# Tile addresses and the transposition of probabilities in a retention and sparse-attention block

## The chip, the cores and the metric

The kernel runs on one core of a Trainium2 chip. Its time is the device time of one execution in microseconds; several executions are taken, and the median counts. Beside it a hardware profile of one execution shows what each engine did: TensorE (PE, with its weight loads as PEld), VectorE (DVE), ScalarE (ACT), GpSimd (POOL), and the DMA queues that SyncE (SP) and POOL feed.

## The reference, cut to what matters

One block of a model: a feed-forward half step, a mixer, a second feed-forward half step, on 16 meta tokens and 512 tokens of 1024 channels, in float32. The mixer adds two branches, each through a sigmoid gate: retention (4 heads, values of 512 channels) and attention (8 heads of 128) over 16 meta keys and the keys that an index picks.

```
def hybrid_mixer(u, pos, k_top, w_in, w_ret_out, w_att_out, w_mix_out):
    ...
    yr = retention(rq.transpose(0, 2, 1, 3), rk.transpose(0, 2, 1, 3), rv.transpose(0, 2, 1, 3))
    yr = yr.transpose(0, 2, 1, 3).reshape(B, T, RET_V)
    yr = (jax.nn.silu(rg) * yr) @ w_ret_out
    ...
    ya = dsa_attention(aq, ak, av, iq, ik, iw, k_top).reshape(B, T, ATT_W) @ w_att_out
    merged = jax.nn.sigmoid(g_ret) * yr + jax.nn.sigmoid(g_att) * ya
    return merged @ w_mix_out
...
        # dsa_attention, one block of queries
        s_meta = jnp.einsum('bqhd,bmhd->bhqm', qb, k_meta).astype(jnp.float32) * scale
        s_meta = jnp.where((meta_pos[None, :] <= tq[:, None])[None, None], s_meta, -jnp.inf)
        s_sel = jnp.einsum('bqhd,bqkhd->bhqk', qb, k_sel).astype(jnp.float32) * scale
        s_sel = jnp.where(sel_ok[:, None], s_sel, -jnp.inf)
        p = jax.nn.softmax(jnp.concatenate([s_meta, s_sel], axis=-1), axis=-1).astype(v.dtype)
        return (jnp.einsum('bhqm,bmhd->bqhd', p[..., :N_META], v_meta)
                + jnp.einsum('bhqk,bqkhd->bqhd', p[..., N_META:], v_sel))
```

## The kernel before, in words

Every large product is made of three: each float32 operand is split into a high part (`split`, L116: an ACT copy to the type fp32r) and a low part (L118: a DVE subtraction), and high x high, high x low and low x high are summed in PSUM (`mm3`, L142 to 157). Weights come by SP's queue into `raw`, and are split into `whi` (ACT) and `wlo` (DVE), each with three buffers.

The order of the work on TensorE is written out by hand: it is the order of the calls. In the attention heads the order on ACT, DVE and POOL is decided when the program is built, by a scheduler that places each instruction; inside a block `with tc.manual_schedule(engines=BUSY)` it is that of the calls too.

Retention keeps its tiles in the pool `rt` (opened at L1807): values `vo`, decayed scores `ph` and `pl`, and two tiles of tails, `vtail` and `ptail`, which hold the last 16 keys stacked for one product. Its weighted sums are `pspv` (L1476 to 1484) and its output projection `psro`. `gap(p, n)` (L273) puts a spacer of n floats into a pool, so that what follows it starts further on; `tails` (L1304) allocates the two tails.

Attention keeps its tiles in the pool `at`. The keys are counted with the 16 meta keys first, the queries without them; so a block of 128 keys, kb, is seen by the queries from 16 before its own block of 128 on. `KQ = [0, 112, 240, 256, 496]` gives the first query column that is kept for each kb: 512, 400, 272, 256 and 16 columns. For every head, in this order on TensorE:

- `score` (L1882): the scores `psS` of four blocks of queries, then DVE's reduction, ACT's exponential into `prob[j]`, and DVE's scaling. `prob[j]` holds 128 queries by 128(j+2) keys; its columns past the last admissible key are zeroed once, when it is allocated.
- `proj_q`, `proj_k`: the next head's queries and keys (`psaq`, `psak`, then `aq`, `ak`).
- `transpose_p` (L1913): the probabilities are turned, keys to partitions, into PSUM (`psPT`, four buffers shared with other small tiles), and split into `pth` and `ptl`. For kb the blocks j = kb-1 to 3 are turned, 13 in all; the block j = kb-1 has only its last 16 queries by 16 keys different from zero among the columns kept. A fourteenth turns the last 16 keys of j = 3, which go to `ptail` (`split_rows`, L1322 to 1326: two ACT copies and a DVE subtraction).
- `wide_gate`: the 24 products of a gate (`psgate`, later `psga`), which need the weights just split.
- `weigh_v` and `weighted` (L1476 to 1484): `psao`, twelve products of v with `pth`, `ptl`, `pth` for kb = 0 to 3, and one with `ptail`. Its result is split into the output `vo` of the pool `ao`, which the output projection `psat` reads after the last head.

Of the kernel before, what the change touches and what calls it, by code (L numbers as in the profile page):

```python
# [11 lines left out]
F32 = mybir.dt.float32  # L12
F32R = mybir.dt.float32r
# [5 lines left out]
P = 128  # L19
D = 1024  # L20
KD = D // P
S = 512
NM = 16
T = S + NM
# [24 lines left out]
KQ = [0, 112, 240, 256, 496]  # L49
# [32 lines left out]
def kernel(ctx: ExitStack, tc: tile.TileContext, x, meta, g1, wg1, wu1, wd1, gm,  # L82
                      w_in, w_ro, w_ao, w_mo, g2, wg2, wu2, wd2, gf, rope, decay, causal, out):
    nc = tc.nc
# [9 lines left out]
    def pool(name, bufs=1, space=None, side=None):  # L94
        kw = {} if space is None else {"space": space}
        if side is not None:
            kw["side"] = side
        return tc.tile_pool(name=name, bufs=bufs, reuse_waits="tile", **kw)
# [6 lines left out]
    ident = cpool.tile([P, P], F32, name="ident")  # L105
# [10 lines left out]
    def split(src, hi, lo, eng=nc.vector):  # L116
        nc.scalar.activation(hi, src, AF.Copy)  # L117
        eng.tensor_tensor(lo, src, hi.bitcast(F32), ALU.subtract)  # L118
# [85 lines left out]
    tp = {}  # L204
# [43 lines left out]
    def wide(n):  # L248

        return -(-n // 64) * 64  # L250
# [22 lines left out]
    def gap(p, n):  # L273

        nc.gpsimd.memset(p.tile([P, n], F32, tag=f"gap{n}", name="gap"), 0.0)
# [257 lines left out]
    def sm_tile(name):  # L533
        return mx["sm"].tile([P, S], F32, tag="sm", name=name)

    def mm_tile(name):
        return mx["mm"].tile([P, 1024], F32, tag="mm", name=name)
# [761 lines left out]
    def stacked(p, name, n):  # L1299
        t = p.tile([P, n], F32R, tag=name, name=name)  # L1300
        nc.gpsimd.memset(t[:TR].bitcast(F32), 0.0)
        return t

    def tails(p, n):  # L1304

        tp.update(v=stacked(p, "vtail", S), p=stacked(p, "ptail", n))
# [13 lines left out]
    def split_rows(src, t, order):  # L1320

        nc.scalar.activation(t[:NM], src, AF.Copy)  # L1322
        at = [32 * i for i in range(1, 3) if order[i] == "h"][0]
        nc.scalar.activation(t[at : at + NM], src, AF.Copy)
        at = 32 * order.index("l")
        nc.vector.tensor_tensor(t[at : at + NM], src, t[:NM].bitcast(F32), ALU.subtract)
# [26 lines left out]
    if True:  # L1353
# [393 lines left out]
        p = RH - 1  # L1747
# [20 lines left out]
        for h in range(1, RH):  # L1768
            gates = gates_of(h)
            n = 4 - (h == p)  # L1770
# [35 lines left out]
        rts = ExitStack()  # L1806
        rt = rts.enter_context(pool("rt"))  # L1807
        tp.update(pool=rt, bufs=4)
        gap(rt, 16)
        tails(rt, 64)  # L1810
        ia, ib = (rt.tile([P, 4, S], F32, tag=f"vo{i}", name="ixs") for i in range(2))
        ka, kb_ = tmp(), tmp()
# [9 lines left out]
        for c in range(2):  # L1822
            t = rt.tile([P, S], F32, tag="sg", name="gate", bufs=4)
# [17 lines left out]
    with pool("ao") as ao:  # L1841
        vo = [ao.tile([P, AH, S], F32R, tag=f"vo{i}", name="vo") for i in range(2)]
        ao_parts = [(vo[0][:, c, :], vo[1][:, c, :]) for c in range(AH)]
        with pool("at") as at:
# [3 lines left out]
            prob = []  # L1848
            for j in range(4):
                wj = min(P * (j + 2), T)  # L1850
                pj = at.tile([P, wj], F32, tag=f"pj{j}", name=f"pj{j}")
                if j < 3:
                    nc.gpsimd.memset(pj[:, NM + P * (j + 1) :], 0.0)
                prob.append(pj)
            tails(at, 48)
            cq, ck = (Cols(w_in, o_ + P, AH - 1, step=1) for o_ in (OFF_AQ, OFF_AK))
            scale = DH**-0.5

# [24 lines left out]
            def score(j, q, k):  # L1883
                n = NM + P * (j + 1)
                qs = slice(j * P, (j + 1) * P)
                if j < 3:
                    ps = sm_tile("psS")
                    outs = [(ps[:, : max(n, 256)], slice(0, max(n, 256)))]
                    sv = ps[:, :n]
                else:  # L1890
                    outs, sv = halves(mm_tile("psS3"))
                for i, (a, b) in enumerate(((q[0], k[0]), (q[0], k[1]), (q[1], k[0]))):
                    for o_, sl in outs:
                        nc.tensor.matmul(o_, a[:, qs], b[:, sl], start=i == 0, stop=i == 2)
                s = tmp()
                m = at.tile([P, 4], F32, tag="stat", name="stat", bufs=8)
                nc.vector.tensor_tensor_reduce(s[:, :n], sv, bias[j], 1.0, MARK, ALU.add,
                                               ALU.max, m[:, 0:1])
                nc.vector.tensor_scalar(m[:, 1:2], m[:, 0:1], -scale, None, ALU.mult)
                nc.scalar.activation(prob[j][:, :n], s[:, :n], AF.Exp, bias=m[:, 1:2], scale=scale,  # L1900
                                     accum_out=m[:, 2:3])

                def to_one():
                    nc.vector.reciprocal(m[:, 3:4], m[:, 2:3])
                    nc.vector.tensor_scalar(prob[j][:, :n], prob[j][:, :n], m[:, 3:4], None, ALU.mult)

                return to_one

            def scores(q, k):
                for j in (2, 1, 0, 3):  # L1910
                    score(j, q, k)()

            def transpose_p():  # L1913
                parts = []
                for kb in range(4):
                    ps = sm_tile("psPT")
                    for j in range(max(kb - 1, 0), 4):
                        nc.tensor.transpose(ps[:, j * P : (j + 1) * P], prob[j][:, kb * P : (kb + 1) * P], ident)
                    if kb == 3:
                        nc.tensor.transpose(ps[:NM, 0:P], prob[3][:, 4 * P : T], ident)  # L1920
                    n = S - KQ[kb]
                    ph = at.tile([P, wide(n)], F32R, tag=f"pth{kb}", name="pth")[:, :n]
                    pl = at.tile([P, wide(n)], F32R, tag=f"ptl{kb}", name="ptl")[:, :n]
                    if kb == 3:
                        split_rows(ps[:NM, P - NM : P], tp["p"][:, :NM], "hlh")
                    split(ps[:, KQ[kb] :], ph, pl)
                    parts.append((ph, pl))
                return parts

            def weigh_v(h, parts, v):  # L1930
                ps = mm_tile("psao")[:, :S]
# [11 lines left out]
            with tc.manual_schedule(engines=BUSY):  # L1943
                w = gr.next()
                k, q = rope_k(first_k, nc.vector), rope_q(first_q, nc.vector)
                t, t5 = (at.tile([P, S], F32, tag="gate", name="gate", bufs=2) for _ in range(2))
                nc.scalar.activation(t, first_gate, AF.Sigmoid)
                gate_acc(4, t)
                ps = mm_tile("psgate")[:, :S]
# [8 lines left out]
            for h in range(AH):  # L1958
                more = h + 1 < AH
                if h:  # L1960
                    scores(q, k)
                if more:
                    q, k = proj_q(w if h == 0 else None), proj_k()
                else:
                    wide_gate(sm_tile("psga"))
                    wide_gate()
                pt = transpose_p()
                wide_gate()
                weigh_v(h, pt, vs[h])
                if h == 1:  # L1970
                    with tc.manual_schedule(engines=BUSY):
                        more_vs = split_values(raw, [v[:, 4:, :] for v in vo])
                if h == 3:
                    place_tails(5)
                    vs += more_vs
# [6 lines left out]
        with pool("ou") as ou:  # L1982
# [6 lines left out]
            for c in range(KD):  # L1989
                w = cols.next()  # L1990
                ps = sm_tile("psat")
                mm3([(ps, slice(0, S))], w, lambda k: ao_parts[k], KD)
                if c < n_left:
                    t = ou.tile([P, S], F32, tag="sa", name="sa", bufs=3)
                    nc.scalar.dma_start(t, gd[KD + c])
                else:
                    t = sa[c - n_left]
# [12 lines left out]
    with pool("om") as ou:  # L2010
# [11 lines left out]
        for c in range(KD):  # L2022
# [3 lines left out]
            ps = sm_tile("psmo")  # L2026
# [254 lines left out]
```

## Time and profile before

| | us |
|---|---|
| median of three runs (1521.64 to 1523.09) | 1522.1 |
| the profiled execution | 1523.13 |
| its span in the trace | 1521.4 |
| PE busy | 1512.0 (99%) |
| PEld busy | 1369.5 (90%) |
| DVE busy | 1094.6 (72%) |
| ACT busy | 725.1 (48%) |
| POOL busy | 103.8 (7%) |
| the attention heads, in the trace | 910 to 1076 |

Times in the trace are counted from the start of the span. A matmul's start is when it begins; its end is modelled, since matmuls overlap in the array, so that the pace of a chain is read from start to start. A row of the timeline gives start, duration, engine, line, operation, written and read tiles, shape, and in brackets how long the engine sat idle before it and who ended that. The chain is a list of pieces: start, length, engine, tile, line and how many instructions.

### The profile page before, as it was taken

What the parts mean: (1) busy time and instruction counts of PE and PEld (TensorE: products, weight loads), DVE (VectorE), ACT (ScalarE), POOL (GpSimd) and SP (SyncE); (2) the same over time, 40 slices, a digit from 0 to 9 for tenths busy, and PEclk for the clock granted to TensorE, in tenths of its full rate; (3) what the DMA queues carried; (4) which work ended last, traced back from release to release, by engine and by line L of the source; (5) the groups of instructions that cost most, each with busy time, mean ns of one, the idle gap of its engine ahead of it and who ended that gap; (6) DMA issues with size and microseconds to landing.
All of it is one profiled execution on the core that took longest, in us unless ns stands there. A gap on an engine that the chain in (4) does not pass through costs nothing.

```text
span 1521.4 us, 23948 instructions
## 1 busy us (share of the span) xinstructions
PE 1512.0 (99%) x9797; PEld 1369.5 (90%) x9797; DVE 1094.6 (72%) x1679; ACT 725.1 (48%) x1132; POOL 103.8 (7%) x133
## 2 busy tenths in 40 slices
PE   9999999999999999999999999999999999999997
PEld 8999999999988888789888888998888899899996
DVE  4988586786886767787878787666455888586675
ACT  5655263454354444543334357666345445254453
POOL 1000000003101120000000021110002000000000
PEclk9999999999999999999999999999999999999999
DMA  5132323226554444232322233233433223233232
GB/s 168 58 121 89 118 90 111 91 92 211 191 167 162 165 146 142 86 122 85 112 82 85 96 118 94 78 88 109 148 131 131 83 84 106 89 111 111 84 124 84
DMA packets 151742, 173.50 MB, mean 114 GB/s; under 512 B 4944, under 2 KB 123240, under 8 KB 150992
## 3 DMA queue, kind: packets, MB, share of 16 engines
q1 hardware_dynamic: 142992, 151.58, 30.7%
q0 software_dynamic: 3808, 11.38, 2.0%
q10 hardware_dynamic: 4832, 9.00, 1.7%
q8 instruction: 77, 1.26, 0.3%
q14 instruction: 33, 0.27, 0.1%
HBM read 155.94 MB, written 16.01 MB: 113 GB/s over the span
## 4 chain that ended last, share of the span: by engine, by line
PE 99%; issue 0%; ACT 0%; DVE 0%; POOL 0%; POOLq 0%
PE psqX L157 14%; PE psd L157 8%; PE psd L2116 8%; PE psqY L157 7%; PE psrg L157 6%; PE psro L157 6%; PE psvX L1135 4%; PE psqZ L157 3%; PE psrk L157 3%; PE psak L157 3%; PE psu L157 3%; PE psrq L157 3%; PE psaq L157 3%; PE psga L157 3%; PE psat L157 3%; PE psmo L157 3%
## 5 line engine op out<-in xcount | busy, mean ns | idle before, releaser
L285 DVE TENSOR_TENSOR wlo<-raw,whi 128x1024 fp32r<-128x1024 f32 (+2 forms) x184 | 198.8, 1084 | 42.4 <-ACT whi L284 42.4
L284 ACT ACTIVATE whi<-raw 128x1024 fp32r<-128x1024 f32 (+2 forms) x184 | 169.8, 924 | 123.3 <-PE psd L157 41.3
L157 PE MATMUL psqX<-tl,whi 128*128 128x264 f32 (+1 forms) x432 | 122.3, 283 | 0.0
L157 PE MATMUL psqX<-th,whi 128*128 128x264 f32 (+1 forms) x432 | 122.3, 283 | 0.0
L157 PE MATMUL psqX<-th,wlo 128*128 128x264 f32 (+1 forms) x432 | 122.2, 283 | 0.0
L118 DVE TENSOR_TENSOR wlo<-raw,whi 128x1024 fp32r<-128x1024 f32 (+1 forms) x60 | 73.6, 1226 | 54.3 <-ACT whi L117 51.8
L284 ACT ACTIVATE whi<-wsum 128x1024 fp32r<-128x1024 f32 x72 | 76.3, 1060 | 70.7 <-PE psd L2116 22.0
L117 ACT ACTIVATE whi<-raw 128x1024 fp32r<-128x1024 f32 (+1 forms) x60 | 62.3, 1043 | 87.8 <-PE psat L157 26.6
L285 DVE TENSOR_TENSOR wlo<-wsum,whi 128x1024 fp32r<-128x1024 f32 x72 | 87.8, 1221 | 12.5 <-ACT whi L284 12.5
L157 PEld LDWEIGHTS psqX<-th,whi 128*128 128x128 f32 x432 | 82.1, 190 | 0.1
L157 PEld LDWEIGHTS psqX<-th,wlo 128*128 128x128 f32 x432 | 82.0, 190 | 0.0
L157 PEld LDWEIGHTS psqX<-tl,whi 128*128 128x128 f32 x432 | 82.0, 190 | 0.0
L157 PE MATMUL psro<-vo,whi 128*128 128x512 f32 x256 | 79.4, 391 | 0.0
L157 PE MATMUL psd<-hl,whi 128*128 128x264 f32 x352 | 71.4, 284 | 0.0
L157 PE MATMUL psd<-hh,wlo 128*128 128x264 f32 x352 | 70.8, 283 | 0.0
L157 PE MATMUL psd<-hh,whi 128*128 128x264 f32 x352 | 70.6, 282 | 0.0
L2116 PE MATMUL psd<-wlo,hh 128*128 128x512 f32 (+1 forms) x182 | 69.3, 382 | 0.0
L2116 PE MATMUL psd<-whi,hh 128*128 128x512 f32 (+1 forms) x182 | 69.2, 382 | 0.0
L2116 PE MATMUL psd<-whi,hl 128*128 128x512 f32 (+1 forms) x182 | 69.2, 382 | 0.0
L157 PEld LDWEIGHTS psro<-vo,whi 128*128 128x128 f32 x256 | 48.1, 188 | 10.3
L157 PEld LDWEIGHTS psd<-hh,wlo 128*128 128x128 f32 x352 | 54.5, 188 | 0.0
L157 PEld LDWEIGHTS psd<-hh,whi 128*128 128x128 f32 x352 | 54.1, 188 | 0.0
(451 smaller groups left out, 4514.4 us busy)
## 6 DMA issues: line engine op xcount, KB each, us to landing
raw<-in_ffn_w_up_dram SPq DMA_DIRECT2D x22, 1024.0 KB, 4.9
raw<-in_ffn_w_gate_dram SPq DMA_DIRECT2D x21, 1024.0 KB, 5.0
raw<-in_w_in_dram SPq DMA_DIRECT2D x18, 1024.0 KB, 5.0
raw<-in_w_in_dram SPq DMA_DIRECT2D x33, 512.0 KB, 3.5
raw<-in_ffn_w_down_dram SPq DMA_DIRECT2D x24, 512.0 KB, 4.2
w<-in_w_in_dram SPq DMA_DIRECT2D x24, 512.0 KB, 6.2
raw<-in_ffn_w_down_dram SPq DMA_DIRECT2D x12, 768.0 KB, 4.3
raw<-in_w_ret_out_dram SPq DMA_DIRECT2D x8, 1024.0 KB, 4.8
```

Of the source, the lines that this page charges most:

```text
L117: nc.scalar.activation(hi, src, AF.Copy)
L118: eng.tensor_tensor(lo, src, hi.bitcast(F32), ALU.subtract)
L157: nc.tensor.matmul(o, a[:, k, :], b[:, sl], start=first and k == 0 and i == 0, stop=last and k == nk - 1 and i == 2, skip_group_check=onto)
L284: nc.scalar.activation(hi, src, AF.Copy)
L285: return lambda: nc.vector.tensor_tensor(lo, src, hi.bitcast(F32), ALU.subtract)
L1135: nc.tensor.matmul(d[bank_][t], a, b[:, k, :], start=not onto and j + k + m == 0, stop=j + k == 3 and m == 2, skip_group_check=onto)
L2116: nc.tensor.matmul(ps, a[:, bs], m[:, j, cs], start=first and i == 0, stop=last and i == 2)
```

## The change

The tiles of both pools start at multiples of 256 bytes: the spacer of 16 floats ahead of retention's tails goes, and in `at` a spacer of 48 floats comes ahead of the tails (whose second tile is now 64 wide) and one of 16 behind the tiles `pth` and `ptl`. The moving operands of `psro`, `pspv` and `psao`, among others, change address by that and keep their shape.

In `transpose_p` the block j = kb-1 is no longer turned by a transposition of 128x128. Its 16x16 that count come as a float32 product of 16 columns of `prob[kb-1]` with 16 columns of the identity, into the first 16 partitions and columns of `psPT`; so do the last 16 keys of j = 3. A head then has 10 transpositions and 4 products in place of 14 transpositions. `pth` and `ptl` are allocated once for all heads and the columns ahead of the block kb are zeroed once (six memsets on POOL); the three memsets of `prob` go. For kb = 1, 2, 3 the split is made in two: 384, 256 or 128 columns, and 16x16. So each head has three more instructions on ACT and three on DVE.

In the built program, heads 1 to 6 have these orders on the two engines. Before, ACT: pth 512, 400, 272, ptail twice, ak, pth 256, whi, table load, gate. DVE: ptl 512, 400, 272, ak, ptail, ptl 256, wlo, scores. After, ACT: pth 512, 384, 256, ptail twice, ak, pth 16x16 twice, pth 128, whi, pth 16x16, table load, gate. DVE: ptl 512, 384, 256, ak, ptl 16x16 twice, ptail, ptl 128, wlo, ptl 16x16, scores. TensorE's order is the same but for the products named.

```
@@ rt pool
         tp.update(pool=rt, bufs=4)
-        gap(rt, 16)
         tails(rt, 64)
@@ at pool
                 pj = at.tile([P, wj], F32, tag=f"pj{j}", name=f"pj{j}")
-                if j < 3:
-                    nc.gpsimd.memset(pj[:, NM + P * (j + 1) :], 0.0)
                 prob.append(pj)
-            tails(at, 48)
+            gap(at, 48)
+            tails(at, 64)
@@ transpose_p
+            parts_p = []
+            for kb in range(4):
+                n = S - KQ[kb]
+                pair = [at.tile([P, wide(n)], F32R, tag=f"pt{c}{kb}", name=f"pt{c}")[:, :n] for c in "hl"]
+                if kb:
+                    for t in pair:
+                        nc.gpsimd.memset(t[:, : P * kb - KQ[kb]].bitcast(F32), 0.0)
+                parts_p.append(pair)
+            gap(at, 16)
+
             def transpose_p():
-                parts = []
+                small = slice(P - NM, P)
                 for kb in range(4):
                     ps = sm_tile("psPT")
-                    for j in range(max(kb - 1, 0), 4):
+                    for j in range(kb, 4):
                         nc.tensor.transpose(ps[:, j * P : (j + 1) * P], prob[j][:, kb * P : (kb + 1) * P], ident)
+                    if kb == 0:
+                        split(ps, *parts_p[0])
+                        continue
+
+                    nc.tensor.matmul(ps[:NM, :NM], prob[kb - 1][:, kb * P : kb * P + NM], ident[:, small], start=True, stop=True)
                     if kb == 3:
-                        nc.tensor.transpose(ps[:NM, 0:P], prob[3][:, 4 * P : T], ident)
-                    n = S - KQ[kb]
-                    ph = at.tile([P, wide(n)], F32R, tag=f"pth{kb}", name="pth")[:, :n]
-                    pl = at.tile([P, wide(n)], F32R, tag=f"ptl{kb}", name="ptl")[:, :n]
-                    if kb == 3:
-                        split_rows(ps[:NM, P - NM : P], tp["p"][:, :NM], "hlh")
-                    split(ps[:, KQ[kb] :], ph, pl)
-                    parts.append((ph, pl))
-                return parts
+                        nc.tensor.matmul(ps[:NM, P : P + NM], prob[3][:, 4 * P : T], ident[:, small], start=True, stop=True)
+                        split_rows(ps[:NM, P : P + NM], tp["p"][:, :NM], "hlh")
+                    a = P * kb - KQ[kb]
+                    split(ps[:, kb * P :], *(t[:, a:] for t in parts_p[kb]))
+                    split(ps[:NM, :NM], *(t[:NM, a - NM : a] for t in parts_p[kb]))
+                return parts_p
```

## The prediction

> **What bounds the kernel now.** I read the shares and the chain of the page first, then the waits of the stage that the change edits (the eight attention heads, 910 to 1076 us), then its timeline.
>
> ```profile
> PE 1512.0 (99%) x9797; PEld 1369.5 (90%) x9797; DVE 1094.6 (72%) x1679; ACT 725.1 (48%) x1132; POOL 103.8 (7%) x133
> ...
> PE 99%; issue 0%; ACT 0%; DVE 0%; POOL 0%; POOLq 0%
> ```
>
> TensorE is busy for 99% of 1521.4 us and is 99% of the chain that ended last, so a time changes only if TensorE issues less, issues at another pace, or waits. In the edited stage:
>
> ```profile
> 890.00:1076.00 186.00, 185.80 (x1111) 166.50 (x1110) 124.92 (x288) 124.41 (x224) 25.87 (x21) 1.00 0.33 96
> ```
>
> ```profile
> ACT pth L117 <- DVE ptail L1326: 7.4, 7, 1.1
> ...
> PEld psao L1483 <- DVE ptl L118: 0.4, 1, 0.4
> ```
>
> The first row is PE, PEld, DVE, ACT, POOL busy, then granted clock (1.00), DMA share and GB/s. DVE and ACT have room (125 of 186 us). The waits are in us, times, longest: TensorE waited for a piece of the probabilities once in eight heads. So the question is not how much DVE and ACT do, but when the piece that TensorE wants next is ready. That is read from the timeline of one head (h = 1):
>
> ```profile
> 939.44 0.16 DVE L1326 TENSOR_TENSOR ptail<-psPT,ptail 16x16 fp32r<-16x16 f32 x1
> ...
> 939.70 0.38 ACT L117 ACTIVATE pth<-psPT 128x256 fp32r<-128x256 f32 x1 [1.06 <-DVE ptail L1326]
> ...
> 940.04 0.39 PE L157 MATMUL psgate<-xl,whi 128*128 128x512 f32 x1
> ...
> 940.11 0.42 DVE L118 TENSOR_TENSOR ptl<-psPT,pth 128x256 fp32r<-128x256 f32 x1 [0.51 <-ACT pth L117]
> ...
> 940.50 0.39 PE L1483 MATMUL psao<-pth,vo 128*128 128x512 f32 x1
> ...
> 940.52 1.06 ACT L117 ACTIVATE whi<-raw 128x1024 fp32r<-128x1024 f32 x1 [0.44 <-PE psgate L157]
> ...
> 941.38 0.34 PE L1483 MATMUL psao<-ptl,vo 128*128 128x400 f32 x1
> ...
> 941.61 1.23 DVE L118 TENSOR_TENSOR wlo<-raw,whi 128x1024 fp32r<-128x1024 f32 x1 [1.08 <-ACT whi L117]
> ...
> 942.13 0.19 PEld L1483 LDWEIGHTS psao<-ptl,vo 128*128 128x128 f32 x1
> ...
> 942.24 0.28 PE L1483 MATMUL psao<-ptl,vo 128*128 128x256 f32 x1
> ```
>
> Three things are to be seen. The last low piece of the head, ptl 128x256 of block kb = 3, is done at 940.53 and used at 942.13: 1.6 us of slack. Right behind it DVE subtracts the next weights (wlo, 941.61 to 942.84), and that cannot go earlier: it waits for ACT's whi (940.52 to 941.58), which waits for a buffer that TensorE's gate products free at 940.43 (940.04 + 0.39). And TensorE wants the last piece in the middle of wlo. The sixth of these heads stands the same:
>
> ```profile
> 1052.30 1.06 ACT L117 ACTIVATE whi<-raw 128x1024 fp32r<-128x1024 f32 x1 [0.41 <-PE psga L157]
> ...
> 1053.39 1.23 DVE L118 TENSOR_TENSOR wlo<-raw,whi 128x1024 fp32r<-128x1024 f32 x1 [1.05 <-ACT whi L117]
> ...
> 1053.91 0.19 PEld L1483 LDWEIGHTS psao<-ptl,vo 128*128 128x128 f32 x1
> ```
>
> **The change, part by part.**
>
> **1. The order of the pieces: +5.0 us.** The split of kb = 1, 2, 3 becomes two: one of 384, 256 or 128 columns, and one of 16x16. In the built program of the changed kernel the 16x16 pieces of kb = 1 and 2 stand ahead of whi (ACT) and wlo (DVE) in heads 1 to 6, and the pieces of 128 columns too, but the 16x16 piece of kb = 3 stands behind both: ACT runs pth 128, whi, pth 16x16, table load, gate; DVE runs ptl 128, wlo, ptl 16x16, and only then the reduction of the next head's scores. The product psao with ptl 128x256 of kb = 3 reads that tile and waits for the last writer. So per head:
> - whi starts when the gate product frees its buffer, unchanged; wlo ends at 942.84 as before.
> - ptl 16x16 starts as the pieces on DVE overlap: in head 0 below, ptl starts 0.09 before the end of the wlo ahead of it (918.17 + 1.22 = 919.39; 919.30). So 942.75; it takes 0.16 (ptail row): done at 942.91.
> - TensorE follows as it does there: ptl done at 919.72, weight load at 919.77, next load at 919.88 where the product begins, so 0.16 later: 943.07. The product stood at 942.24. That is 0.83 a head, x 6 = 5.0. ACT's piece of kb = 3 ends near 941.75 (whi's end + 0.16, the ptail row's length) and is wanted one product ahead of ptl, near 942.1: in time.
>
> Lower end: without the exposed load it is 942.96 - 942.24 = 0.72, x 6 = 4.3. Upper: 0.1 more for the hand-over from ACT, 5.6. I take 5.0, since head 0 shows this very wait:
>
> ```profile
> 918.17 1.22 DVE L118 TENSOR_TENSOR wlo<-raw,whi 128x1024 fp32r<-128x1024 f32 x1
> ...
> 919.30 0.42 DVE L118 TENSOR_TENSOR ptl<-psPT,pth 128x256 fp32r<-128x256 f32 x1
> ...
> 919.64 1.22 DVE L118 TENSOR_TENSOR vo<-vraw,vo 128x1024 fp32r<-128x1024 f32 x1
> 919.77 0.19 PEld L1483 LDWEIGHTS psao<-ptl,vo 128*128 128x128 f32 x1 [0.41 <-DVE ptl L118]
> ...
> 919.88 0.19 PEld L1483 LDWEIGHTS psao<-pth,vo 128*128 128x128 f32 x1
> ...
> 920.12 0.17 PE L1484 MATMUL psao<-ptail,vtail 80*128 80x16 f32 x1
> ...
> 920.15 0.43 PE L1894 MATMUL psS<-ak,aq 128*128 128x400 f32 x1
> ```
>
> Behind the waiting product TensorE has four short ones of this head and then the scores of the next; DVE's reductions of those scores and ACT's gate move with it. TensorE has no idle time later in the head that could take the 0.83 back. On ACT the table load and the gate come 0.16 later while TensorE comes 0.83 later, so whoever takes the gate's PSUM buffer next has gained time: priced at nothing, the cover being the wait itself.
>
> Head 0 waits already. There DVE gets three more pieces (about 0.1 each as they overlap, 0.3), two of them ahead of the last ptl, and its big piece shrinks from 256 to 128 columns. I take +0.2 (0 to 0.4). Head 7 has no wlo at this place and I price it at nothing.
>
> **2. Transposes and products: +0.2 us.**
>
> ```profile
> 933.65 1.42 PE psPT L1918 x13
> 935.08 0.11 PE psPT L1920
> ...
> 940.66 1.98 PE psao L1483 x12
> ```
>
> A transposition costs 1.42 / 13 = 0.109, a head 1.53. After: 10 transpositions, 1.09; 4 products of 16 columns. The nearest product is the 16-column psao with ptail above: the next starts 0.03 behind it (920.12, 920.15), but that one lasts 0.43 where psao's 400 columns take 0.34, since its weights could not load behind so short a product: 0.09. With two passes per fp32 product (an estimate; no row of before shows such a product) it is 4 x 2 x 0.027 = 0.21, and three loads of 128 columns are left exposed (behind kb = 1, 2 and ahead of the gate): 3 x 0.08 = 0.24. Sum 1.54 to 1.55, so +0.02 a head, +0.2 in eight. Lower end, loads all hidden: 1.31, -0.2 a head, -1.7 in all. Upper end, passes twice as dear: +0.2 a head, +1.7. The three memsets of pj that go and the six of pt that come are on POOL ahead of the first head, where POOL is busy for 25.87 of 186 us.
>
> **3. Alignment: -1.0 us.**
>
> ```profile
> 646.01 21.99 PE psro L157 x96
> ```
>
> ```profile
> 1076.44 43.67 PE psat L157 x192
> ```
>
> ```profile
> 592.42 1.98 PE pspv L1483 x12
> ```
>
> psro and psat have the same shape, 512 moving columns of vo. In psro those tiles begin 64 bytes past a multiple of 256, in psat at one: 21.99 / 96 = 229.1 ns against 43.67 / 192 = 227.4. The change puts psro's tiles at multiples: 384 x 1.7 = 0.65. pspv, 192 products in 16 dozens, moves ph and pl from the same pool; at 1.7 each, 0.33. Its lower end is the aligned pace for all its columns: a dozen has 3 x (512 + 400 + 272 + 256) = 4320, at 227.4 / 512 = 0.444 ns is 1.92, so 0.06 a dozen, 1.0 in all. psao's tiles gain as much per head, but in heads 0 to 6 that only lengthens the wait of step 1. So -1.0, from 0 to -1.7.
>
> On this term the Trainium skill speaks otherwise: "SBUF — State Buffer", section "Door 1: The DMA port swizzle", gives lines of 16 bytes as what an access can lose by crossing. By that rule 64 bytes past a multiple is already aligned and this term is nothing; the rows above, 229.1 against 227.4, speak mildly against it, though psro and psat stand in different stages.
>
> **Sum:** 5.0 + 0.2 + 0.2 - 1.0 = +4.4. The profiled execution spans 1521.4 and took 1523.13, its work around the span 1.7; the three runs lie at 1521.64, 1522.1 and 1523.09, so it is 1.0 above their median. I add to the median: 1522.1 + 4.4 = **1526.5 us**.
>
> **Rivals.**
> - **No wait appears, not slower.** If the last 16x16 piece were ready at 942.08, only 0.2 - 1.0 would be left: 1521.3. For that whi would have to begin 0.83 earlier, at 939.69; but ACT's own pth of kb = 3 starts at 939.70 and the gate product holds whi's buffer until 940.43. Half the wait gone would still leave 2.5 - 0.6 = +1.9. Against it: both rows; for it only that a piece of 128 columns ends sooner than one of 256. Chance 0.10.
> - **The alignment brings nothing**, psro's 1.7 ns being the stage's and not the address's: 1522.1 + 5.4 = 1527.5. For it: no product was seen at both addresses. Chance 0.13.
> - **The small products are dear** (the upper end of step 2): +1.5 more, 1528.0. Chance 0.08.
> - **The small products are cheap and alignment reaches its far end**: 4.3 + 0.2 - 1.7 - 1.7 = +1.1, 1523.2. Chance 0.08; with more than this from neighbouring tiles it would be faster, a further 0.04.
>
> **How the numbers follow.** The forecast has 0.57. About 0.2% (3.0 us) is what a measurement of this kernel can tell from no change, so slower means above 1525.1: of the forecast 0.52 lies there, with 0.13 and 0.08 that is 0.73. Same: 0.05 of the forecast, 0.08 of the first rival, 0.08 of the cheap one, 0.21. Faster: 0.02 of the first rival and 0.04, 0.06. The range leaves out the first rival and most of the ends: from the cheap case with part of its bound, 1522.9, to the dear one with the wait at its upper end (1528.0 + 0.6), 1528.6.
>
> **What would show it.** Step 1: TensorE waits at psao for DVE's ptl seven times instead of once, about 0.7 to 0.8 each, with a 16x16 piece right behind wlo. Step 2: the stretch from the first transposition to the first gate product about 1.55. Step 3: psro's 96 products in 21.83 instead of 21.99, pspv's dozen in 1.96. I would be wrong most of all if wlo ends earlier than 942.8 of this head, or if the product does not wait for the 16x16 piece.

## The result, and the profile after

The changed kernel takes 1529.79 us (median of five runs, 1529.23 to 1530.60) against 1522.15 before; the ratio is 1.0050, interval 1.0038 to 1.0061: slower by 7.6 us. Timed again beside another kernel it took 1530.54 against 1522.51, ratio 1.0052 (1.0040 to 1.0065). The forecast was 1526.5, range 1522.9 to 1528.6. The direction was right, and the time lies outside the range.

The page of the changed kernel, busy time and the chain that ended last:

```profile
PE 1516.1 (99%) x9829; PEld 1369.6 (90%) x9829; DVE 1093.6 (72%) x1703; ACT 727.9 (48%) x1156; POOL 103.7 (7%) x137
...
PE 98%; DVE 1%; ACT 1%; issue 0%; POOL 0%; POOLq 0%; ACTq 0%
```

TensorE is still the bound, but DVE and ACT, 0% of the chain before, now hold 1% each: TensorE waits for them. Where it waits is in the list of waits of the attention heads (us, times, longest):

```profile
PEld psao L1483 <- DVE ptl L118: 4.8, 6, 0.8
...
PEld psPT L1933 <- issue: 2.7, 16, 0.2
```

The first row is the wait that was forecast, once in each of six heads. The second was not forecast: in each head the weight loader stands idle 0.17 ahead of two loads of the small products (and 0.12 ahead of a third), for nothing that the profile shows. Both are in the chain of the head h = 1 (start, length, what):

```profile
932.50 0.76 PE psPT L1928 x7
933.27 0.14 PE psPT L1933 x2
933.41 0.37 PE psPT L1928 x2
933.78 0.14 PE psPT L1933 x2
933.92 0.26 PE psPT L1928
934.18 0.14 PE psPT L1933 x2
934.33 0.05 PE psPT L1935 x2
934.38 5.45 PE psgate L157 x23
...
939.90 1.07 ACT whi L117
...
940.99 1.23 DVE wlo L118
942.22 0.08 DVE ptl L118
942.30 0.04 issue
942.35 0.50 PE psao L1483 x2
```

Before, this head went from the transpositions (1.42 + 0.11) to the gate (5.48) and psao (1.98) without leaving TensorE. Now the transpositions and products take 1.88, and the chain leaves TensorE at the gate's last but one product for whi, wlo and the 16x16 ptl. Measured from start to start of TensorE's instructions, the change of each stretch is (rounded, so that the differences add to 7.5):

| stretch | before | after | difference |
|---|---|---|---|
| start of the span to the first transposition | 910.65 | 909.34 | -1.3 |
| transpositions and products, eight heads | 1.447 each | 1.967 each | +4.2 |
| gate products behind them, eight heads | 44.42 in all | 44.62 in all | +0.2 |
| psao, heads 1 to 6 | 2.011 each | 2.840 each | +5.0 |
| psao, head 0 | 2.479 | 1.990 | -0.5 |
| all the rest | | | -0.1 |
| span | 1521.4 | 1528.8 | +7.4 |

So two new costs of about equal size, one of which had been priced at +0.2.

### The profile page after: what moved, and what is told of

Same layout as the page of the kernel before. It is cut to its first block, busy times and chain, and to the rows that moved or that the text cites. A ratio compares the mean times of both kernels' runs of the same rounds, so it can differ in the third digit from the quotient of the medians.

```text
span 1528.8 us, 24067 instructions
## 1 busy us (share of the span) xinstructions
PE 1516.1 (99%) x9829; PEld 1369.6 (90%) x9829; DVE 1093.6 (72%) x1703; ACT 727.9 (48%) x1156; POOL 103.7 (7%) x137
## 4 chain that ended last, share of the span: by engine, by line
PE 98%; DVE 1%; ACT 1%; issue 0%; POOL 0%; POOLq 0%; ACTq 0%
PE psqX L157 14%; PE psd L157 8%; PE psd L2128 8%; PE psqY L157 7%; PE psrg L157 6%; PE psro L157 6%; PE psvX L1135 4%; PE psqZ L157 3%; PE psrk L157 3%; PE psak L157 3%; PE psu L157 3%; PE psrq L157 3%; PE psgate L157 3%; PE psga L157 3%; PE psaq L157 3%; PE psat L157 3%
```

## Experiments

Runs of the kernel before beside these had a median of 1522.4 to 1522.5 us. "The stretch" is the time from the first transposition of a head to its first gate product; before it is 1.447 us, after 1.967. In the shape of a matmul's row the stationary operand, which a weight load (PEld) brings in, stands first (`128*16`) and the moving one behind it (`128x16`). A float32 product shows as two loads and two matmuls; they are called its two passes here.

**The addresses alone, and the products alone.** The first kernel is that of before with the new addresses, the second the changed one at the old addresses.

```
@@ e1_align, against the kernel before
-        gap(rt, 16)
         tails(rt, 64)
...
-            tails(at, 48)
+            gap(at, 48)
+            tails(at, 64)
+            gap(at, 16)
@@ e2_products_only, against the changed kernel
+        gap(rt, 16)
         tails(rt, 64)
...
-            gap(at, 48)
-            tails(at, 64)
+            tails(at, 48)
...
+            gap(at, 48)
             parts_p = []
```

> The kernel before with the new addresses alone (retention's spacer dropped; in the attention pool spacers of 48 and 16 floats around the tails, so that the tails, pth, ptl, aq and ak start at multiples of 256 bytes); transpositions and splits stay those of before. Theory: the first transposition of the trace came 1.3 us earlier after the change (909.34 against 910.65), all of it from addresses, and psao and the rest gain another 0.1 to 0.3: 1520.6 (1520.3 to 1521.0). Rival, that the addresses bring nothing and the 1.3 us had another cause: 1522.2.

> The changed kernel at the addresses of before: only the small products and the split in two. Theory: the time of the changed kernel plus what the addresses bring, 1529.8 + 1.5 = 1531.3. Rival, addresses bring nothing: 1529.8. If the wait for the last 16x16 piece or the longer stretch of transpositions came from the new addresses, it would fall towards 1526.

Measured: 1521.15 (ratio 0.9992, 0.9983 to 1.0001) and 1531.57 (1.0058, 1.0045 to 1.0071). The addresses bring 1.3 us by the medians in the one case, though that interval reaches 1 and the time lies 0.15 above the range expected; without them the changed kernel is 1.8 above its first median (1529.79), 1.0 above its second (1530.54). The medians alone would not settle it. The traces do: from retention's first psrg product to the first transposition TensorE takes 355.7 and 355.8 us in the two kernels at the old addresses, and 354.5 to 354.6 in all ten profiles at the new ones, 1.2 less. Three quarters of that are one group of instructions, psro's products, here 96 of them in the chain of the changed kernel and of the one with the old addresses:

```profile
646.00 21.76 PE psro L157 x96
```

```profile
645.46 21.99 PE psro L157 x96
```

At multiples of 256 bytes a product takes 21.76 / 96 = 226.7 ns, 64 bytes further 229.1, exactly as before the change; of what such a product reads, the edit moves only the pool of its moving operand, vo. Four such chains make 0.9 us. The two kernels also show that neither new cost comes from the addresses: at the old ones the stretch is 1.967 and psao 2.83 to 2.84 just the same.

**The small split first.**

```
-                    split(ps[:, kb * P :], *(t[:, a:] for t in parts_p[kb]))
                     split(ps[:NM, :NM], *(t[:NM, a - NM : a] for t in parts_p[kb]))
+                    split(ps[:, kb * P :], *(t[:, a:] for t in parts_p[kb]))
```

> The changed kernel with the two splits of a block in the other order, 16x16 first; in the built program the last pieces of kb = 3 then stand ahead of whi and wlo in heads 1 to 6. Theory: the wait of 0.83 us in six heads goes, the stretch of transpositions and products stays at 1.97 a head: 1529.8 - 5.0 = 1524.8 (1524.3 to 1525.3). Rival, that the wait only moves to the 128-column piece, or comes back elsewhere: 1528 or more.

Measured: 1524.99 (ratio 1.0015, 1.0006 to 1.0024), 4.8 us below the changed kernel. The stretch stayed at 1.967 and psao fell from 2.840 to 1.990. The timeline of head 1 in this kernel:

```profile
938.65 0.29 DVE L118 TENSOR_TENSOR ptl<-psPT,pth 128x128 fp32r<-128x128 f32 x1 [0.34 <-ACT pth L117]
...
940.20 1.23 DVE L118 TENSOR_TENSOR wlo<-raw,whi 128x1024 fp32r<-128x1024 f32 x1 [1.26 <-ACT whi L117]
...
940.69 0.19 PEld L1483 LDWEIGHTS psao<-ptl,vo 128*128 128x128 f32 x1
```

The last piece is now the 128-column one; it ends at 938.94, ahead of wlo, and TensorE takes it at 940.69 without waiting, while wlo still runs. Two lines exchanged places, no work was saved, and 4.8 us went: the wait was a matter of order alone.

**One change of kind in place of three.** All four products of a head stand behind its ten transpositions.

```
                 for kb in range(4):
                     ...
                     for j in range(kb, 4):
                         nc.tensor.transpose(ps[:, j * P : (j + 1) * P], prob[j][:, kb * P : (kb + 1) * P], ident)
+                for kb in range(1, 4):
+                    nc.tensor.matmul(pss[kb][:NM, :NM], prob[kb - 1][:, kb * P : kb * P + NM], ident[:, small], start=True, stop=True)
+                nc.tensor.matmul(pss[3][:NM, P : P + NM], prob[3][:, 4 * P : T], ident[:, small], start=True, stop=True)
...
```

> The changed kernel with the four products of a head behind all ten transpositions instead of between them; ACT's and DVE's order is unchanged, so the wait of 0.83 us stays. Theory: what is dear is each change between a transposition and a float32 product of 16 columns (some 0.09 going in and 0.1 coming out, while nothing is loaded ahead), so with one change in place of three the stretch falls from 1.97 to about 1.5 us a head: 1529.8 - 8 x 0.47 = 1526.0. Rival, that the products themselves are dear wherever they stand: 1.97 stays, 1529.8.

Measured: 1527.36 (ratio 1.0031, 1.0019 to 1.0042). The stretch fell to 1.480, as the theory gave; the time is 1.4 above its figure because head 0 waited again (psao 2.450 against 1.990, and 0.15 in what follows it), which the theory had not counted, and some 0.7 is left. In the two profiles nothing is left (the span is 3.6 shorter: 3.9 from the stretch and 0.3 ahead of the heads, less the 0.6 of head 0), and the changed kernel's own two medians are 0.75 apart. The chain of head 1 shows what the products themselves cost:

```profile
932.27 1.09 PE psPT L1930 x10
933.36 0.25 PE psPT L1932 x6
933.61 0.05 PE psPT L1933 x2
```

Eight passes, 0.30 with the one change into them; in a row a pass costs 0.025. From one change to three the stretch grows by 0.487, so 0.24 for a change there and back.

**What makes a change dear.** Two kernels keep the products between the transpositions and alter the product: one takes 128 stationary columns instead of 16, still float32; the other stays at 16 columns but in fp32r, one pass.

```
@@ e5_wide_products, against the changed kernel
-  nc.tensor.matmul(ps[:NM, :NM], prob[kb - 1][:, kb * P : kb * P + NM], ident[:, small], ...)
+  nc.tensor.matmul(ps[:, :NM], prob[kb - 1][:, kb * P : (kb + 1) * P], ident[:, small], ...)
...
@@ e7_fp32r_products, against the changed kernel
-  pj = at.tile([P, wj], F32, tag=f"pj{j}", name=f"pj{j}")
+  pj = at.tile([P, wj], F32R, tag=f"pj{j}", name=f"pj{j}")
-  ... ident[:, small], ...
+  ... ident_r[:, small], ...
```

> The changed kernel with the three products of kb = 1, 2, 3 made from 128 columns of the probabilities instead of 16 (the same float32 product, 128 stationary and 16 moving columns; the columns beyond the 16 give rows that nobody reads); the tail's product becomes a transposition again. In the built program the last pieces stand ahead of whi and wlo, so heads 1 to 6 have no wait. Theory: the change between a transposition and a float32 product is dear only where the product's stationary operand is narrow; with 128 columns a product costs about what a transposition does, the stretch is about 1.55 us a head and the time 1525.0 (the kernel with 16x16 first) - 8 x 0.42 + 0.3 for head 0's wait = 1521.9. Rival, that each change between the two kinds of instruction is dear whatever the width: the stretch stays at 1.9 or more, 1525 or more.

> The changed kernel with the four products in fp32r (one pass) instead of float32 (two passes), at the same places and widths; the probabilities are for that rounded to fp32r when they are scaled, which changes the computation a little. The order on ACT and DVE is unchanged, so the wait of 0.83 us in six heads stays. Theory: the two-pass product with a narrow stationary operand is what drains the array; in one pass, as in retention's 16-column psst, nothing drains: stretch about 1.45, 1529.8 - 8 x 0.52 + 0.5 (head 0 waits again) = 1526.1. Rival, that any narrow product between transpositions drains: 1.9 a head, 1529.8.

Measured: 1522.48 (ratio 1.0001, 0.9992 to 1.0010) with a stretch of 1.61, and 1524.91 (1.0016, 1.0007 to 1.0025) with a stretch of 1.27. Neither rival stands, though both stretches missed their figures: 1.55 and 1.45 were expected, so that the first kernel is 0.6 us slower and the second 1.2 faster than its theory. The weight loads tell it, first those of the changed kernel, then of the wide float32 product, then of the narrow fp32r product; all are the first change of head 1:

```profile
932.67 0.60 PE L1928 MATMUL psPT<-ident,pj 128*128 128x128 f32 x4
933.20 0.21 PE L1933 MATMUL psPT<-ident,pj 128*16 128x16 f32 x2
```

```profile
933.20 0.11 PEld L1933 LDWEIGHTS psPT<-ident,pj 128*16 128x16 f32 x2 [0.17 <-issue]
933.34 0.20 PEld L1928 LDWEIGHTS psPT<-ident,pj 128*128 128x128 f32 x2
```

```profile
932.65 0.14 PEld L1930 LDWEIGHTS psPT<-ident,pj 128*128 128x128 f32 x1
932.76 0.30 PEld L1935 LDWEIGHTS psPT<-ident,pj 128*128 128x128 f32 x2
```

```profile
932.61 0.10 PEld L1935 LDWEIGHTS psPT<-ident_r,pj 128*16 128x16 f32 x1
932.64 0.25 PE L1935 MATMUL psPT<-ident_r,pj 128*16 128x16 f32 x1
```

In the changed kernel the load of the small product begins at 933.20, 0.2 after the last transposition's start (four of them from 932.67, 0.109 apart, so 932.99), and so 0.09 after the next transposition would have begun. With 128 columns, or in one pass, the load of the product begins right behind the start of the matmul ahead of it (932.65 to 932.76 is the pace of the transpositions) and no idle time stands before it. From start to start, at the same place in the three kernels:

| us | transposition to product | first to second pass | product to transposition | that one to the next |
|---|---|---|---|---|
| changed kernel | 0.203 | 0.039 | 0.106 | 0.165 |
| 128 stationary columns, float32 | 0.110 | 0.030 | 0.112 | 0.143 |
| 16 stationary columns, fp32r | 0.029 | | 0.109 | 0.142 |

The way out is alike in all three; it is on the way in that they part. So it is neither the change of kind nor the narrow operand nor the two passes by themselves, but the narrow operand in a two-pass float32 product. That the array runs empty there, as the theory has it, no run shows.

The Trainium skill ("TensorE: Matmul & The Clock Gate", Part 2, "Step-by-step: what each phase is for") has weight loads pulled ahead of running matmuls where row groups don't conflict or a background buffer is the target. The transpositions agree with it: each load starts 0.002 us behind the start of the matmul ahead. Ahead of the first pass of a narrow float32 product the trace shows that this pulling ahead stops (0.2 us behind that start); the page does not speak of that case.

**Both costs lowered.** The first kernel, e8, joins the two edits above, the grouped products and the small split first. The second, e9, has the small split first and all fourteen transpositions, four of them of 16 stationary columns:

```
@@ e9_transposed_small_first, against e3_small_first
-  nc.tensor.matmul(ps[:NM, :NM], prob[kb - 1][:, kb * P : kb * P + NM], ident[:, small], start=True, stop=True)
+  nc.tensor.transpose(ps[:NM, (kb - 1) * P : kb * P], prob[kb - 1][:, kb * P : kb * P + NM], ident)
...
```

> The four products behind the transpositions and the 16x16 splits ahead of the wide ones: both costs of the change that were found are reduced at once. Theory: the two add, stretch 1.48 and no wait: 1525.0 - 8 x 0.487 = 1521.1 (1520.7 to 1521.7). Rival, that one brings the other back: 1524 or more.

> The new addresses and the split in two, 16x16 first, but all fourteen transpositions again, the small ones of 16 stationary columns. Theory: no change of kind, stretch 1.45 as before, no wait in any head, head 0 included, where the kernel with the addresses alone still waits 0.34: 1521.15 - 0.4 = 1520.8 (1520.4 to 1521.2), the fastest of all. Rival, that the three more splits a head cost something elsewhere: 1521.2 or more.

Measured: 1521.20 (ratio 0.9992, 0.9984 to 1.0001) and 1520.75 (0.9990, 0.9981 to 0.9998). The two remedies add, and e9 is just clear of the kernel before. One thing was missed: head 0 still waits some 0.2 to 0.3 in both (psao 2.184 and 2.277, against 1.990 without a wait). So e9 met its figure by luck in part: 0.4 was to come from head 0's wait against the kernel with the addresses alone, and 0.06 came (2.333 to 2.277). That e9 is faster than that kernel is not shown, since their intervals overlap.

**A version that keeps the small products and gains.** The 16 columns of each block are split into a high and a low part beforehand, and both go through one-pass products into one sum, behind the ten transpositions.

```
+                corner = [at.tile([P, 4 * NM], F32R, tag=f"co{c}", name=f"co{c}") for c in "hl"]
+                for i in range(4):
+                    split(prob[i][:, (i + 1) * P : (i + 1) * P + NM], *(t[:, i * NM : (i + 1) * NM] for t in corner))
...
+                    for c in range(2):
+                        nc.tensor.matmul(dst, corner[c][:, i * NM : (i + 1) * NM], ident_r[:, small], start=c == 0, stop=c == 1)
```

> New addresses, 16x16 splits first, and the four small blocks as one-pass fp32r products behind the ten transpositions, each as two products, of the high and the low part of its 16 columns (eight more small instructions a head on ACT and DVE together, during the next head's projections). Theory: ten transpositions at 0.109 and eight one-pass products at 0.026 give a stretch of 1.30 a head against 1.447 with fourteen transpositions, 0.15 x 8 = 1.2 less than that kernel's 1520.75: 1519.6 (1519.2 to 1520.2). Rival, that the eight small instructions delay the next weights' split, which stands behind them, and TensorE waits for it: 1520.8 or more.

> The changed kernel once more, timed on the chip and in the rounds of the run beside it. Theory: 1529.8, 1.0048 to 1.005 of the kernel before.

Measured: 1520.01 (ratio 0.9984, 0.9975 to 0.9993) beside 1530.54 for the changed kernel in the same rounds (0.7 above its figure; ratio 1.0052). This chain of head 1 has nothing but TensorE in it:

```profile
931.64 1.09 PE psPT L1935 x10
932.73 0.20 PE psPT L1939 x8
932.93 5.58 PE psgate L157 x24
938.50 1.96 PE psao L1483 x12
```

The stretch is 1.306, as given; the eight further small splits a head bring no new wait (head 0's psao takes 2.260, near e9's). By its median it is the fastest of all, 2.5 us below before, though its interval overlaps e9's.

## Why the prediction was right or wrong

- **Step 1, the order of the pieces: right, in place and size.** 0.83 a head was forecast by laying head 0's wait over the other heads, and psao grew by 2.840 - 2.011 = 0.829. The row in the changed kernel is the one that was described: the 16x16 ptl right behind wlo, TensorE behind it.

```profile
940.99 1.23 DVE L118 TENSOR_TENSOR wlo<-raw,whi 128x1024 fp32r<-128x1024 f32 x1 [1.71 <-ACT whi L117]
...
942.13 0.15 DVE L118 TENSOR_TENSOR ptl<-psPT,pth 16x16 fp32r<-16x16 f32 x1
...
942.35 0.19 PEld L1483 LDWEIGHTS psao<-ptl,vo 128*128 128x128 f32 x1 [0.80 <-DVE ptl L118]
```

- **Step 1, head 0: wrong in sign, small.** +0.2 was forecast, and its wait went (-0.5). TensorE reaches psao 0.5 later there, because of step 2, so that the longer order of pieces is ready. In the second profile of the same kernel 0.1 of the wait is left (psao 2.097), and in the kernels where the stretch is short again, head 0 waits again (2.184 to 2.606).
- **Step 2, transpositions and products: this is the step that failed.** +0.02 a head was forecast, with +0.2 as its upper end; it is +0.52. The passes had been priced rightly (0.027, measured 0.025), and so had the load behind a product (0.027 + 0.08, measured 0.106). Two things were wrong. The way into the product was put at nothing: its load starts 0.09 after the next transposition would have begun, three times a head (0.28), and the transposition behind each of the first two products takes 0.06 more before the next instruction starts (0.165 instead of 0.109; 0.11 a head). And the 1.53 for before counts the last transposition with 0.11, while the gate's product starts 0.03 behind it: the stretch was 1.447, so that the forecast stretch of 1.55 was itself +0.10 a head, +0.8 in eight. In all eight heads the stretch brings +4.2, and with the gate's first products +4.4, against +0.2: 4.2 us, more than the whole error of 3.3.
- **The reason it was missed is in the prediction's own sentence, that no row of before shows such a product.** One did. The kernel before has narrow float32 products elsewhere, psvl, with 32 stationary columns, and its timeline shows the very gap:

```profile
425.58 0.39 PE L1135 MATMUL psvZ<-whi,xl 128*128 128x512 f32 x1
...
425.81 0.39 PE L1135 MATMUL psvZ<-wlo,xh 128*128 128x512 f32 x1
426.13 1.14 PEld L1098 LDWEIGHTS psvl<-w,xlast 128*32 128x32 f32 x44 [0.35 <-issue]
```

  A product of 512 columns goes on after 0.23 (425.58, 425.81), so the load should have started with it at 425.81 and its matmul at 426.04; the load started at 426.13, 0.09 after that, as at the transpositions. psvl differs, since its products write four groups of 32 partitions in turn, so the row suggests the price and does not prove it. The psao product with ptail, which was used in its place, is one-pass with 128 stationary columns, and lacks just what made the price.
- **Step 3, the addresses: right in the sum, in part by luck.** -1.0 was forecast, and from retention's first product to the first transposition it is -1.2. psro gained 0.9, more than its 0.65; pspv gained 0.13 in place of 0.33, for its thirteen products took 2.001 to 2.013 before and 1.990 to 2.020 after, some of them longer; other products gained 0.2 on balance, which had not been counted. By the Trainium skill's lines of 16 bytes ("SBUF — State Buffer", section "Door 1: The DMA port swizzle"), as the prediction applied them, the term would be nothing; 229.1 against 226.7 at the same product decides against that.
- **The rivals.** No wait: refuted by the six waits. Addresses bring nothing: refuted by psro at both addresses. Dear products: the time went this way, at two and a half times the rival's price and not for its reason, passes twice as dear. The range ended at 1528.6 because its end was made from dearer passes and had no term for the way in.

## What to carry to other kernels

Before an instruction is called new to a kernel, search the trace for its kind by operand type and width, not by its line: the one row that prices it may stand in another stage, and an idle time put down to issue in front of a weight load is such a price. Splitting a piece in two is only harmless if both halves keep their place ahead of the next long instruction on that engine; here two exchanged lines were worth 4.8 us. A small product between transpositions saves nothing if it stops the loading ahead: group such products, or make them one-pass.

## What the runs showed that was not expected

- A float32 product of 16 stationary columns between transpositions costs about 0.24 us there and back, though its two passes take 0.05; the same product with 128 stationary columns, or with 16 in fp32r, shows no idle time ahead of its load. Why the hardware does this was not settled; that the three conditions belong together is what e4, e5 and e7 show.
- A moving operand of 512 float32 columns that starts 64 bytes past a multiple of 256 costs 229.1 ns against 226.7.
- The start of the attention heads moved by up to 0.8 us between kernels with the same instructions ahead of it (908.66 to 909.43), so that differences of some tenths were read from stretches between TensorE's own starts and not from the position in the span. That scatter lies ahead of retention, whose first product starts anywhere from 554.1 to 554.9.
